# A gated-delta mixer: key norms from squares summed on TensorE ahead of the transposes, and raised priorities in the sample output

## The chip, the cores and the metric

The kernel runs on one core of a Trainium2 chip. A core has five engines with a queue of instructions each: TensorE (PE in the profile, its weight loads PEld), VectorE (DVE), ScalarE (ACT), GpSimd (POOL) and SyncE (SP), which here only issues DMAs. An engine runs its queue strictly in order and waits on semaphores for what other engines have to deliver. The metric is device time in microseconds (us) of one launch, as the median of several runs.

## The reference

The reference is one step of a small recurrent decoder trunk: two layers, each a feed-forward block, a mixer and a second feed-forward block, over 256 prompt tokens and 8 sequences of 8 sample tokens. The mixer's gated delta rule needs the keys normalised to unit length:

```python
def l2norm(x):
    return x * lax.rsqrt(jnp.sum(x * x, axis=-1, keepdims=True) + EPS)
...
    q = l2norm(qkv[:, :, 0]) * (DN_HEAD_DIM ** -0.5)
    k = l2norm(qkv[:, :, 1])
    v = qkv[:, :, 2]
    beta = jax.nn.sigmoid(scal[..., :DN_HEADS])
...
    kbeta = kb * bb[..., None]
    A = jnp.where(strict, jnp.einsum('nbhid,nbhjd->nbhij', kbeta, kb) * decay, 0.0)
...
        v_new = uc - jnp.einsum('bhcd,bhde->bhce', wc, S)
        o = jnp.einsum('bhcd,bhde->bhce', qc * jnp.exp(Gc)[..., None], S) + jnp.einsum('bhij,bhje->bhie', ac, v_new)
        gl = Gc[..., -1]
        S = S * jnp.exp(gl)[..., None, None] + jnp.einsum('bhcd,bhce->bhde', kc * jnp.exp(gl[..., None] - Gc)[..., None], v_new)
...
    o = rmsnorm(o, dn_norm_w) * jax.nn.silu(gates[..., RG_WIDTH:].reshape(B, L, DN_HEADS, DN_HEAD_DIM))
```

There are 4 heads of 128 columns; `g` are the decays, `G` their running sums, `o` the output that a second norm scales.

## The kernel before

All 320 tokens lie along the free dimension, the features on the 128 partitions. A product with a weight is done in three matmuls, since each operand is split into a rounded high part and a rest (`xh`, `xl`, `wh`, `wl`): L153, `Unit.mm`, eight blocks of 128 rows to a unit. A unit's weights come by one DMA (L117); ScalarE makes the high part (L125) and VectorE the rest (L130, the weight split).

TensorE's order is written out by hand. In the mixer the small dependent steps of the delta rule stand between pieces of the projections: `F(n)` issues the next n matmuls of the weight units as filler, `F.to(i)` those up to unit i, and the lists `FL`, `FZ`, `FY` hold the counts. When a unit is done, its `done` function reads its PSUM buffer out (a convolution for `k`, `q`, `v`: L667 and L668 on VectorE, then L677, L679, L700). There are three PSUM buffers for units (`mm`), four for the small steps (`sm`) and one for sums (`st`, the tile `ssp`).

The order on the other engines is made by a scheduler from priorities; `with tc.high_priority(offset=HPO)` (HPO is 400) puts what it holds ahead of other work. The order that it makes is fixed when the program is built, so an instruction that waits holds up all that stand behind it on its engine.

The steps that the change touches, in the order of the program, once in each layer:

- decays: TensorE's `gp` (L789 to L794) gives the running sums `G`; `gr` (L813, L816) gives them along rows; VectorE forms the differences `DN` (the program's `Dp`, L821) and `Ds` (L824), and ScalarE takes exponentials (L829 to L835);
- `tok`: TensorE transposes the keys (L850) in three groups, ScalarE squares each of ten blocks with its accumulator giving the sum of squares (L854), then copies the blocks scaled into `kd` (L858);
- norms: VectorE adds EPS (L868), GpSimd raises to the power -1/2 (L869), VectorE forms `dd` and `negc` (L870, L871), and later L872 and L873;
- `kk` and `kks`: products of keys (L885, L890), which VectorE scales into `nA` and `nAs` (L914, L921) for the triangular solve. Its steps are called `quads` (L907): TensorE multiplies, VectorE copies with a predicate (L1012) and transposes. The products for the queries (`kq_prep`) and the sums of `q` (L776) lie among them;
- output: `scale_o` squares `por` (its tile is `qa`), VectorE and GpSimd form the factor `fs` (L1050, L1051), ScalarE scales (L1056). For the sample tokens VectorE first adds `pso` and `kso` (L1158), which frees the PSUM buffer `pso`;
- state update: two halves of four products (L1194), each with the four `sm` buffers, and VectorE adds them to the state (L1197). Between the halves six matmuls of the next unit stand (`F(FL[19])`). After it the output is transposed (L1206).

A token (`self.token`, L722) is a tile of zeros that is handed on as a bias, to hold ScalarE's use of another function table until a certain step is done.

Of the kernel before, what the change touches and what calls it, by code (L numbers as in the profile page):

```python
# [11 lines left out]
AF = mybir.ActivationFunctionType  # L12
OP = mybir.AluOpType
# [13 lines left out]
EPS = 1e-6  # L27
# [3 lines left out]
HPO = 400  # L31
# [32 lines left out]
def bc(ap, n):  # L64
    return ap.to_broadcast([ap.shape[0], n])
# [11 lines left out]
def trunk(ctx, tc, x_prompt, x_sample, state_conv, state_rglru, state_delta,  # L77
# [6 lines left out]
    act, dve, pe, pool = nc.scalar.activation, nc.vector, nc.tensor, nc.gpsimd  # L84
    stt = dve.scalar_tensor_tensor
# [17 lines left out]
    def smtile():  # L103
        return smp.tile([128, 512], F32, name="sm")
# [504 lines left out]
    class Mixer:  # L609
# [127 lines left out]
        def run(self):  # L737
# [3 lines left out]
            vec, mhalf = C["vec"], C["mhalf"]  # L741
            ka, kas, qa, qas, va, vas = self.ka, self.kas, self.qa, self.qas, self.va, self.vas
# [12 lines left out]
            beta, g, ss, rk, negc, dd, kds, negEG, nk, t0_ = (sv[:, i] for i in range(10))  # L755
# [12 lines left out]
            ssp = sttile()  # L768

            def sumsq_units(c0, src, srcs, hs):  # L770
                for h in hs:
                    if h < NH:
                        s = sqtile()
                        act(s[:, 0:NP], src[:, h], AF.Square)
                        for t in range(2):
                            pe.matmul(ssp[:, c0 + 4 * t + h:c0 + 4 * t + h + 1], s[:, t * 128:(t + 1) * 128],  # L776
                                      ones[:, 0:1], start=True, stop=True)
                    else:
                        sx = tmp.tile([128, NH, 64], F32, name="sqs")
                        act(sx, srcs, AF.Square)  # L780
                        for p in range(2):
                            pe.matmul(ssp[:, c0 + 8 + p:c0 + 9 + p], sx[:, 2 * p:2 * p + 2].rearrange("p a b -> p (a b)"),
                                      ones[:, 0:1], start=True, stop=True)

            F(FL[1])
            self.late_state()
            F(FL[2])
            gp = smtile()
            pe.matmul(gp[:, 0:8], U, g[:, 0:8], start=True, stop=True)  # L789
            pe.matmul(gp[:, 8:10], U8, g[:, 8:10], start=True, stop=True)  # L790
# [6 lines left out]
            eG, eGL, eSel, eKD = GE[:, 0:10], GE[:, 10:20], GE[:, 20:52], GE[:, 52:62]  # L797
# [10 lines left out]
            for t in range(2):  # L808
                gr = smtile()
                grs.append(gr)  # L810
                for h in range(NH):
                    u = 4 * t + h
                    pe.matmul(gr[:, h * 128:(h + 1) * 128], bc(g[:, u:u + 1], 128), U, start=True, stop=True)  # L813
            gr = smtile()
            for p in range(2):
                pe.matmul(gr[:, 128 * p:128 * p + 128], bc(g[:, 8 + p:9 + p], 128), U8, start=True, stop=True)  # L816
            with tc.high_priority(offset=HPO):
                for t in range(2):
                    for h in range(NH):
                        u = 4 * t + h  # L820
                        stt(Dp[:, u], grs[t][:, h * 128:(h + 1) * 128], G[:, u:u + 1], mnP, op0=OP.subtract, op1=OP.min)  # L821
                for p in range(2):
                    for h, r in enumerate(HF):
                        stt(Ds[r, p], gr[r, 128 * p + 64 * h:128 * p + 64 * h + 64], G[r, 8 + p:9 + p], mn8[r],  # L824
                            op0=OP.subtract, op1=OP.min)
                if TK:
                    act(GE, GE, AF.Exp)
                else:
                    act(GE, GE, AF.Exp, bias=self.token(Ds[:, 1, 63:64]))  # L829
                dve.tensor_scalar(negEG, eG, -1.0, None, op0=OP.mult)  # L830
                act(Dp[:, 0:4], Dp[:, 0:4], AF.Exp)
                act(Dp[:, 4:8], Dp[:, 4:8], AF.Exp)
                act(Ds, Ds, AF.Exp)
                act(qg[:, :, 0:128], grs[1].rearrange("p (h i) -> p h i", h=NH), AF.Exp)
                act(qg[:, :, 128:192], gr[:, 0:256].rearrange("p (h i) -> p h i", h=NH), AF.Exp)  # L835
                self.tokq = self.token(qg[:, 3, 128:129])

            kd = mt([128, NU, 128], "kd")
            vn = mt([128, NU, 128], "vn")
            qss = mt([128, NU], "qss")  # L840

            def tok(u0, src, srcs, dst, scl, sums=None):
                n = 4 if u0 < 8 else 2
                ps = smtile()
                for i in range(n):
                    if u0 < 8:
                        a = src[:, i, 32 * u0:32 * u0 + 128]
                    else:
                        a = srcs[:, 2 * i:2 * i + 2]
                    pe.transpose(ps[:, i * 128:(i + 1) * 128], a, ident)  # L850
                if sums is not None:
                    with tc.high_priority(offset=HPO):
                        for i in range(n):
                            act(dst[:, u0 + i], ps[:, i * 128:(i + 1) * 128], AF.Square,  # L854
                                accum_out=sums[:, u0 + i:u0 + i + 1])
                for i in range(n):
                    u = u0 + i
                    act(dst[:, u], ps[:, i * 128:(i + 1) * 128], AF.Copy, scale=scl[:, u:u + 1])  # L858
# [3 lines left out]

            F(FL[4])
            for u0 in (0, 4, 8):
                tok(u0, ka, kas, kd, eKD, ss)
                F(FL[5])
            with tc.high_priority(offset=HPO):
                dve.tensor_scalar(ss, ss, EPS, None, op0=OP.add)  # L868
                pool.tensor_tensor(rk, ss, mhalf, op=OP.pow)  # L869
                dve.tensor_mul(dd, beta, rk)  # L870
                stt(negc, dd, -1.0, rk, op0=OP.mult, op1=OP.mult)  # L871
            dve.tensor_mul(dd, dd, rk)  # L872
            dve.tensor_mul(nk, ss, rk)  # L873

            nA = mt([128, 8, 128], "nA")
            at = mt([128, 8, 128], "at")
            nAs = mt([128, 2, 64], "nAs")
# [3 lines left out]
            for t in range(2):  # L881
                tk = slice(t * 128, t * 128 + 128)
                ps = smtile()
# [26 lines left out]
            with tc.high_priority(offset=HPO):  # L910
                for t in range(2):
                    for h in range(NH):
                        u = 4 * t + h
                        stt(nA[:, u], kk[t][:, h * 128:h * 128 + 128], negc[:, u:u + 1], Dp[:, u],  # L914
                            op0=OP.mult, op1=OP.mult)
# [75 lines left out]
            for li, s in enumerate(LEV[1:]):  # L991
# [16 lines left out]
                for a, b in grp:  # L1008
                    n = b - a
# [36 lines left out]
            def scale_o(u0, n):  # L1046
                for i in range(n):
                    act(sqtile()[:, 0:128], por[:, u0 + i], AF.Square, accum_out=oss[:, u0 + i:u0 + i + 1])
                us = slice(u0, u0 + n)
                stt(fs[:, us], oss[:, us], 1.0 / 128, qss[:, us], op0=OP.mult, op1=OP.add)  # L1050
                pool.tensor_tensor(fs[:, us], fs[:, us], mhalf[:, us], op=OP.pow)  # L1051
                for i in range(n):
                    if SO:
                        dve.tensor_scalar(por[:, u0 + i], por[:, u0 + i], fs[:, u0 + i:u0 + i + 1], None, op0=OP.mult)
                    else:
                        act(por[:, u0 + i], por[:, u0 + i], AF.Copy, scale=fs[:, u0 + i:u0 + i + 1])  # L1056
# [98 lines left out]
            for p in range(2):  # L1155
                u = 8 + p
                pe.matmul(pso[:, p * 128:p * 128 + 128], ats[:, p], vn[:, u], start=True, stop=True)
            dve.tensor_add(por[:, 8:10], pso[:, 0:256].rearrange("p (u c) -> p u c", c=128), kso[:, 1])  # L1158
            scale_o(8, 2)

            ves = []
# [251 lines left out]
```

## Time and profile before

| | |
|---|---|
| runs, us | 1306.49 median of 3 (1301.82 to 1308.19) |
| profiled execution, us | 1302.74, of which the span 1301.0 |
| busy: PE / DVE / ACT / POOL | 97% / 68% / 56% / 9% of the span |
| mean granted TensorE clock | 0.984 of full speed |
| HBM traffic | 143 GB/s over the span |

The span goes from the first instruction to the last. A row of a timeline gives the start, the duration, engine, line, operation, the tile written and those read, the shapes and a count; at its end stands, in brackets, how long the engine had been idle before and what released it. Neighbouring rows overlap, since an instruction's end is counted with its drain: what an instruction takes in a row of its kind is the distance from start to start. `sv` in the profile is a small tile for vectors: `ss`, `rk`, `dd`, `negc` and others.

### The profile page before, as it was taken

The numbers are of one execution on the slowest core, as the hardware profiler recorded it, in microseconds if no ns is written. First come the engines' busy times: TensorE is split into PE (matmuls) and PEld (weight loads), VectorE is DVE, ScalarE is ACT, GpSimd is POOL, SyncE is SP. The second block draws the span as 40 slices with busy tenths as digits, with TensorE's granted clock in tenths as the row PEclk, the third lists the DMA queues.
The fourth block names the chain that finished last, engine by engine and source line by source line (L and its number), as shares of the span: only waits on it lengthen the run. The fifth ranks groups of instructions, "written<-read, shape, count | busy, mean of one in ns | idle before, by whom it ended". The sixth has DMA issues, their size and how long they took to land.

```text
span 1301.0 us, 24528 instructions
## 1 busy us (share of the span) xinstructions
PE 1255.6 (97%) x9849; PEld 1220.4 (94%) x9849; DVE 885.6 (68%) x1542; ACT 730.6 (56%) x1216; POOL 117.9 (9%) x243
## 2 busy tenths in 40 slices
PE   7899999999999999999999999999999999999995
PEld 6899999889979999999999999999897899999995
DVE  5977744689777877764487775459995768767443
ACT  5655544575586755544465554446758666555444
POOL 1200000232120100000000000013321110000000
PEclk8999999999989999999999999999999899999998
DMA  7655555563336455555635555575332655555541
GB/s 180 163 160 162 157 154 162 141 163 82 83 96 188 125 163 162 163 150 165 182 105 163 162 162 153 159 200 132 82 87 70 173 143 162 163 162 158 147 134 41
DMA packets 355686, 187.26 MB, mean 144 GB/s; under 512 B 8890, under 2 KB 353292, under 8 KB 355572
## 3 DMA queue, kind: packets, MB, share of 16 engines
q1 hardware_dynamic: 352724, 178.51, 48.7%
q0 software_dynamic: 2672, 6.65, 1.9%
q8 instruction: 77, 1.26, 0.4%
q10 hardware_dynamic: 176, 0.53, 0.1%
q14 instruction: 37, 0.30, 0.1%
HBM read 179.16 MB, written 6.51 MB: 143 GB/s over the span
## 4 chain that ended last, share of the span: by engine, by line
PE 84%; DVE 7%; ACT 5%; DMA 2%; issue 1%; POOL 1%; SPq 0%; ACTq 0%; DVEq 0%
PE mm L153 41%; PE sm L153 35%; PE sm L907 2%; DVE xl L222 2%; ACT xh L221 1%; DMA raw<-in_ffn_w_up_dram 1%; PE st L226 1%; DVE wl L130 1%; ACT wh L125 1%; PE sm L1194 1%; PE sm L971 1%; DVE x L411 1%; DVE xr L1097 0%; ACT hp L1072 0%; DVE co L679 0%
## 5 line engine op out<-in xcount | busy, mean ns | idle before, releaser
L130 DVE TENSOR_TENSOR wl<-raw,wh 128x1024 fp32r<-128x1024 f32 (+1 forms) x322 | 385.3, 1197 | 208.2 <-ACT wh L125 204.2
L125 ACT ACTIVATE wh<-raw 128x1024 fp32r<-128x1024 f32 (+1 forms) x317 | 328.1, 1035 | 342.7 <-issue 130.3
L153 PE MATMUL mm<-xh,wl 128*128 128x320 f32 x976 | 294.4, 305 | 4.9 <-DVE wl L130 4.9
L153 PE MATMUL mm<-xh,wh 128*128 128x320 f32 x976 | 294.9, 305 | 1.1 <-ACT xh L221 1.1
L153 PE MATMUL mm<-xl,wh 128*128 128x320 f32 x976 | 286.7, 303 | 2.1 <-DVE xl L222 2.1
L153 PE MATMUL sm<-xh,wh 128*128 128x320 f32 x720 | 215.6, 299 | 0.0
L153 PE MATMUL sm<-xh,wl 128*128 128x320 f32 x720 | 215.5, 299 | 0.0
L153 PE MATMUL sm<-xl,wh 128*128 128x320 f32 x720 | 215.3, 299 | 0.0
L153 PEld LDWEIGHTS mm<-xh,wl 128*128 128x128 f32 x976 | 185.8, 191 | 7.9 <-DVE wl L130 5.9
L153 PEld LDWEIGHTS mm<-xh,wh 128*128 128x128 f32 x976 | 186.0, 191 | 6.0 <-issue 2.3
L153 PEld LDWEIGHTS mm<-xl,wh 128*128 128x128 f32 x976 | 183.3, 191 | 4.4 <-DVE xl L222 2.4
L153 PEld LDWEIGHTS sm<-xh,wl 128*128 128x128 f32 x720 | 136.1, 189 | 0.0
L153 PEld LDWEIGHTS sm<-xh,wh 128*128 128x128 f32 x720 | 136.1, 189 | 0.0
L153 PEld LDWEIGHTS sm<-xl,wh 128*128 128x128 f32 x720 | 136.1, 189 | 0.0
L153 PE MATMUL sm<-gh,wh 128*128 128x320 f32 x374 | 112.2, 300 | 0.0
L153 PE MATMUL sm<-gh,wl 128*128 128x320 f32 x374 | 111.9, 299 | 0.0
L153 PE MATMUL sm<-gl,wh 128*128 128x320 f32 x374 | 111.8, 299 | 0.0
L153 PE MATMUL mm<-gh,wh 128*128 128x320 f32 x330 | 99.0, 300 | 0.0
L153 PE MATMUL mm<-gh,wl 128*128 128x320 f32 x330 | 98.8, 300 | 0.0
L153 PE MATMUL mm<-gl,wh 128*128 128x320 f32 x330 | 98.7, 299 | 0.0
L497 ACT ACTIVATE gh<-t 128x320 fp32r<-128x320 f32 x88 | 70.0, 805 | 8.2 <-DVE t L495 7.3
L153 PEld LDWEIGHTS sm<-gh,wl 128*128 128x128 f32 x374 | 70.7, 189 | 0.0
(440 smaller groups left out, 2059.8 us busy)
## 6 DMA issues: line engine op xcount, KB each, us to landing
raw<-in_ffn_w_up_dram SPq DMA_DIRECT2D x176, 512.0 KB, 3.9
raw<-in_ffn_w_down_dram SPq DMA_DIRECT2D x64, 512.0 KB, 4.1
raw<-in_w_in_dram SPq DMA_DIRECT2D x48, 512.0 KB, 4.1
raw<-in_ffn_w_down_dram SPq DMA_DIRECT2D x32, 384.0 KB, 3.5
raw<-in_w_out_dram SPq DMA_DIRECT2D x16, 512.0 KB, 3.9
aux<-in_state_delta_dram SPq DMA_DIRECT2D x8, 512.0 KB, 6.5
out_dram<-aux POOLq DMA_DIRECT2D x8, 512.0 KB, 5.7
xtok<-in_x_prompt_dram SPq DMA_DIRECT2D x2, 512.0 KB
```

Source lines behind the costliest of these rows:

```text
L125: act(wh[:, :nk], raw[:, :nk], *((AF.Copy,) if tok is None or tok[0] else (AF.Identity, tok[1]())))
L130: (sub or dve).tensor_sub(wl[:, :nk], raw[:, :nk], wh[:, :nk].bitcast(F32))
L153: pe.matmul(self.blk.ps(), w, il(xx), start=self.first and self.pos == 1, stop=self.last and self.pos == 3 * self.nk)
L221: act(h, pr(x[:, k]), AF.Copy, scale=g)
L222: stt(il(xl[:, k]), pr(x[:, k]), g, h.bitcast(F32), op0=OP.mult, op1=OP.subtract)
L226: pe.matmul(ps[:, t:t + 1], s[:, a:b], ones[:, 0:1], start=start and t == 0, stop=stop, skip_group_check=True)
L411: dve.tensor_add(x[:, k], x[:, k], t)
L497: act(h, pr(t2), AF.Copy)
L907: pe.matmul(ps[HF[h], 64 * i:64 * i + 64], lhs(u, h), rhs(u, h), start=True, stop=True)
L971: pe.matmul(ps[32 * j:32 * j + 32, 128 * i:128 * i + 128], kz[:, h, i, c:c + 32], SS[p][:, j // 2, 4 * (j % 2) + b], start=b == 0, stop=b ...
L1194: pe.matmul(ps2[j], kd[r, u], ve[r], start=True, stop=True)
```

## The change

The sums of squares of the keys are no longer taken by ScalarE's accumulator from the transposed keys. `sumsq_units`, which the kernel already used for `q`, squares the keys as they come (ScalarE, L774 and L780) and sums over the partitions by matmuls with one column of ones. Heads 0 to 2 stand ahead of `gp`, head 3 and the sample tokens behind `gr`. The norms' small operations move up with them. The output factor's two operations and the sample output's add get the raised priority. No line of the diff concerns the state update itself.

```diff
--- before.py
+++ after.py
@@ -785,6 +785,7 @@
             F(FL[1])
             self.late_state()
             F(FL[2])
+            sumsq_units(0, ka, kas, (0, 1, 2))
             gp = smtile()
             pe.matmul(gp[:, 0:8], U, g[:, 0:8], start=True, stop=True)
             pe.matmul(gp[:, 8:10], U8, g[:, 8:10], start=True, stop=True)
@@ -814,6 +815,14 @@
             gr = smtile()
             for p in range(2):
                 pe.matmul(gr[:, 128 * p:128 * p + 128], bc(g[:, 8 + p:9 + p], 128), U8, start=True, stop=True)
+            sumsq_units(0, ka, kas, (3, 4))
+            with tc.high_priority(offset=HPO):
+                dve.tensor_scalar(ss, ssp[:, 0:10], EPS, None, op0=OP.add)
+                pool.tensor_tensor(rk, ss, mhalf, op=OP.pow)
+                dve.tensor_mul(dd, beta, rk)
+                stt(negc, dd, -1.0, rk, op0=OP.mult, op1=OP.mult)
+            dve.tensor_mul(dd, dd, rk)
+            dve.tensor_mul(nk, ss, rk)
             with tc.high_priority(offset=HPO):
                 for t in range(2):
                     for h in range(NH):
@@ -839,7 +848,7 @@
             vn = mt([128, NU, 128], "vn")
             qss = mt([128, NU], "qss")
 
-            def tok(u0, src, srcs, dst, scl, sums=None):
+            def tok(u0, src, srcs, dst, scl):
                 n = 4 if u0 < 8 else 2
                 ps = smtile()
                 for i in range(n):
@@ -848,11 +857,6 @@
                     else:
                         a = srcs[:, 2 * i:2 * i + 2]
                     pe.transpose(ps[:, i * 128:(i + 1) * 128], a, ident)
-                if sums is not None:
-                    with tc.high_priority(offset=HPO):
-                        for i in range(n):
-                            act(dst[:, u0 + i], ps[:, i * 128:(i + 1) * 128], AF.Square,
-                                accum_out=sums[:, u0 + i:u0 + i + 1])
                 for i in range(n):
                     u = u0 + i
                     act(dst[:, u], ps[:, i * 128:(i + 1) * 128], AF.Copy, scale=scl[:, u:u + 1])
@@ -862,16 +866,8 @@
 
             F(FL[4])
             for u0 in (0, 4, 8):
-                tok(u0, ka, kas, kd, eKD, ss)
+                tok(u0, ka, kas, kd, eKD)
                 F(FL[5])
-            with tc.high_priority(offset=HPO):
-                dve.tensor_scalar(ss, ss, EPS, None, op0=OP.add)
-                pool.tensor_tensor(rk, ss, mhalf, op=OP.pow)
-                dve.tensor_mul(dd, beta, rk)
-                stt(negc, dd, -1.0, rk, op0=OP.mult, op1=OP.mult)
-            dve.tensor_mul(dd, dd, rk)
-            dve.tensor_mul(nk, ss, rk)
-
             nA = mt([128, 8, 128], "nA")
             at = mt([128, 8, 128], "at")
             nAs = mt([128, 2, 64], "nAs")
@@ -1047,8 +1043,9 @@
                 for i in range(n):
                     act(sqtile()[:, 0:128], por[:, u0 + i], AF.Square, accum_out=oss[:, u0 + i:u0 + i + 1])
                 us = slice(u0, u0 + n)
-                stt(fs[:, us], oss[:, us], 1.0 / 128, qss[:, us], op0=OP.mult, op1=OP.add)
-                pool.tensor_tensor(fs[:, us], fs[:, us], mhalf[:, us], op=OP.pow)
+                with tc.high_priority(offset=HPO):
+                    stt(fs[:, us], oss[:, us], 1.0 / 128, qss[:, us], op0=OP.mult, op1=OP.add)
+                    pool.tensor_tensor(fs[:, us], fs[:, us], mhalf[:, us], op=OP.pow)
                 for i in range(n):
                     if SO:
                         dve.tensor_scalar(por[:, u0 + i], por[:, u0 + i], fs[:, u0 + i:u0 + i + 1], None, op0=OP.mult)
@@ -1155,7 +1152,8 @@
             for p in range(2):
                 u = 8 + p
                 pe.matmul(pso[:, p * 128:p * 128 + 128], ats[:, p], vn[:, u], start=True, stop=True)
-            dve.tensor_add(por[:, 8:10], pso[:, 0:256].rearrange("p (u c) -> p u c", c=128), kso[:, 1])
+            with tc.high_priority(offset=HPO):
+                dve.tensor_add(por[:, 8:10], pso[:, 0:256].rearrange("p (u c) -> p u c", c=128), kso[:, 1])
             scale_o(8, 2)
 
             ves = []
```

VectorE, layer 0, between the running sums and the next weight split; `sv<-st` (L820) adds EPS to the sums, `sv<-sv` at L822 and L823 are `dd` and `negc`. Before:

```order
L821 SCALAR_TENSOR_TENSOR DN_3175<-sm,G,mnP 128x128 [waits PE_49]
L821 SCALAR_TENSOR_TENSOR DN_3175<-sm,G,mnP 128x128 x3
L821 SCALAR_TENSOR_TENSOR DN_3175<-sm,G,mnP 128x128 [waits PE_49]
L821 SCALAR_TENSOR_TENSOR DN_3175<-sm,G,mnP 128x128 x3
L824 SCALAR_TENSOR_TENSOR Ds<-sm,G,mn_454 64x64 [waits PE_49]
L824 SCALAR_TENSOR_TENSOR Ds<-sm,G,mn_454 64x64 x3
L668 TENSOR_TENSOR cb<-mm,rsb_86 128x8x8
L722 TENSOR_SCALAR tok<-Ds 128x1 [waits DVE_49]
L130 TENSOR_TENSOR wl<-raw,wh 128x1024 [waits DMAHW7_49]
```

and after:

```order
L830 SCALAR_TENSOR_TENSOR DN_3187<-sm,G,mnP 128x128 [waits PE_49]
L830 SCALAR_TENSOR_TENSOR DN_3187<-sm,G,mnP 128x128 x3
L820 TENSOR_SCALAR sv<-st 128x10 [waits PE_49]
L830 SCALAR_TENSOR_TENSOR DN_3187<-sm,G,mnP 128x128
L822 TENSOR_TENSOR sv<-sv 128x10 [waits Pool_49]
L830 SCALAR_TENSOR_TENSOR DN_3187<-sm,G,mnP 128x128
L823 SCALAR_TENSOR_TENSOR sv<-sv 128x10 [waits DVE_49]
L830 SCALAR_TENSOR_TENSOR DN_3187<-sm,G,mnP 128x128 x2
L833 SCALAR_TENSOR_TENSOR Ds<-sm,G,mn_454 64x64 x4
L668 TENSOR_TENSOR cb<-mm,rsb_86 128x8x8
L722 TENSOR_SCALAR tok<-Ds 128x1 [waits DVE_49]
L130 TENSOR_TENSOR wl<-raw,wh 128x1024 [waits DMAHW7_49]
```

The add, `dd` and `negc` now stand inside the row of `DN`; `Ds`, L668, the token and the split L130 stand behind `dd`, which waits for GpSimd.

TensorE, layer 0, the keys' products `kk` (L885 before, L881 after) and the sample tokens' `kks` (L890 before, L886 after). Before:

```order
L885 MATMUL sm<-ka 128x128 [waits PE_49,Activation_49]
L885 MATMUL sm<-ka 128x128 x3
L885 MATMUL sm<-ka 128x128 [waits Activation_49]
L885 MATMUL sm<-ka 128x128 x3
L890 MATMUL sm<-ka 64x64 [waits DVE_49]
L890 MATMUL sm<-ka 64x64 x3
```

and after:

```order
L881 MATMUL sm<-ka 128x128 [waits Activation_49]
L881 MATMUL sm<-ka 128x128 x3
L881 MATMUL sm<-ka 128x128 [waits Activation_49]
L881 MATMUL sm<-ka 128x128 x3
L886 MATMUL sm<-ka 64x64 [waits Activation_49]
L886 MATMUL sm<-ka 64x64 x3
```

`kks` waited for VectorE (the buffer that `nA` reads) and now waits for ScalarE.

VectorE, layer 0, the sample section; `qa<-sm,kso` is the sample output's add, `hp` and `xr` belong to the other recurrence, `aux<-aux,sm` is the state update. Before:

```order
L1097 SCALAR_TENSOR_TENSOR xr<-vo,hp 128x320 [waits DVE_49,Pool_49]
L1090 TENSOR_TENSOR hp<-hp 128x320 [waits Activation_49] x2
L1094 TENSOR_TENSOR hp<-hp,ts__4325 128x8 [waits DVE_49]
L1093 TENSOR_TENSOR ts__4333<-vo,vec 128x8
L1090 TENSOR_TENSOR hp<-hp 128x320 [waits Activation_49]
L1097 SCALAR_TENSOR_TENSOR xr<-vo,hp 128x320 [waits DVE_49,Pool_49]
L1094 TENSOR_TENSOR hp<-hp,ts__4333 128x8 [waits DVE_49]
L1093 TENSOR_TENSOR ts__4341<-vo,vec 128x8
L1158 TENSOR_TENSOR qa<-sm,kso 128x256 [waits PE_49]
L1097 SCALAR_TENSOR_TENSOR xr<-vo,hp 128x320 [waits DVE_49,Pool_49]
L1094 TENSOR_TENSOR hp<-hp,ts__4341 128x8 [waits DVE_49]
L130 TENSOR_TENSOR wl<-raw,wh 128x1024 [waits DMAHW1_49,Activation_49]
```

and after:

```order
L1091 TENSOR_TENSOR hp<-hp,ts__4327 128x8 [waits DVE_49]
L1094 SCALAR_TENSOR_TENSOR xr<-vo,hp 128x320 [waits DVE_49,Pool_49]
L1087 TENSOR_TENSOR hp<-hp 128x320 [waits Activation_49] x2
L1156 TENSOR_TENSOR qa<-sm,kso 128x256 [waits PE_49]
L1091 TENSOR_TENSOR hp<-hp,ts__4335 128x8 [waits DVE_49]
L1090 TENSOR_TENSOR ts__4343<-vo,vec 128x8
L1087 TENSOR_TENSOR hp<-hp 128x320 [waits Activation_49]
L1094 SCALAR_TENSOR_TENSOR xr<-vo,hp 128x320 [waits DVE_49,Pool_49]
L1091 TENSOR_TENSOR hp<-hp,ts__4343 128x8 [waits DVE_49]
L1090 TENSOR_TENSOR ts__4351<-vo,vec 128x8
L130 TENSOR_TENSOR wl<-raw,wh 128x1024 [waits DMAHW1_49,Activation_49]
L1047 SCALAR_TENSOR_TENSOR fs<-oss,qss 128x4 [waits Activation_49]
```

The add has moved up, ahead of four small operations, one of 320 columns and a scan.

## Rows read from the trace of the kernel before

**Rows 1.** TensorE's waits, whole trace: engine, tile, line, releaser: us, times, longest
```profile
PE sm L890 <- DVE nA L914: 4.7, 2, 2.4
PE sm L1194 <- DVE qa L1158: 4.3, 2, 2.2
```

**Rows 2.** TensorE's timeline, layer 0: start, us, engine, line, operation, count, idle before
```profile
281.53 0.38 PE L153 MATMUL mm<-xh,wh 128*128 128x320 f32 x1
...
284.50 0.30 PE L153 MATMUL mm<-xh,wh 128*128 128x320 f32 x1
285.23 0.40 PE L153 MATMUL mm<-xh,wl 128*128 128x320 f32 x1 [0.43 <-DVE wl L130]
...
288.71 2.17 PE L885 MATMUL sm<-ka 128*128 128x128 f32 x16
293.25 0.57 PE L890 MATMUL sm<-ka 128*64 128x64 f32 x8 [2.37 <-DVE nA L914]
...
298.85 1.15 PE L907 MATMUL sm<-Tt,nA 64*64 64x64 f32 x32
```

**Rows 3.** VectorE's timeline, the same stretch
```profile
280.48 2.16 DVE L821 SCALAR_TENSOR_TENSOR DN<-sm,G,mnP 128x128 f32<-128x128 f32 x8
...
283.95 1.22 DVE L130 TENSOR_TENSOR wl<-raw,wh 128x1024 fp32r<-128x1024 f32 x1
...
288.67 0.17 DVE L868 TENSOR_SCALAR sv<-sv 128x10 f32<-128x10 f32 x1
...
291.21 0.19 DVE L870 TENSOR_TENSOR sv<-sv 128x10 f32<-128x10 f32 x1 [1.89 <-POOL sv L869]
...
302.94 0.57 DVE L679 SCALAR_TENSOR_TENSOR co<-cb,vec,co 128x344 f32<-128x344 f32 x1 [0.57 <-ACT co L677]
303.86 0.92 DVE L1012 COPY_PREDICATED Tt<-mT,sm 128x512 f32<-128x512 int32 x2 [0.35 <-PE sm L907]
```

**Rows 4.** GpSimd's timeline, the norms' power
```profile
288.93 2.24 POOL L869 TENSOR_TENSOR sv<-sv,mhalf 128x10 f32<-128x10 f32 x1 [0.67 <-DVE sv L868]
```

**Rows 5.** Windows: us, busy PE, PEld, DVE, ACT, POOL, clock, DMA share, GB/s
```profile
293.00:297.00 4.00, 3.75 (x21) 3.63 (x22) 3.91 (x13) 3.51 (x9) 0.00 (x0) 0.57 0.00 0
303.00:345.00 42.00, 42.00 (x650) 38.67 (x647) 38.98 (x101) 20.37 (x39) 11.46 (x25) 1.00 0.34 90
```

**Rows 6.** TensorE's timeline, four passes of L776 and what follows
```profile
312.72 0.50 PE L776 MATMUL st<-ones,sq 128*128 128x1 f32 x4
313.15 1.08 PE L971 MATMUL sm<-aux,hp 128*32 128x128 f32 x32
```

**Rows 7.** TensorE's timeline, layer 1, the same place as rows 2
```profile
922.63 0.45 PE L890 MATMUL sm<-ka 128*64 128x64 f32 x8 [2.37 <-DVE nA L914]
...
926.60 1.15 PE L907 MATMUL sm<-Tt,nA 64*64 64x64 f32 x32
...
929.08 0.40 PE L153 MATMUL mm<-xh,wl 128*128 128x320 f32 x1 [0.45 <-DVE wl L130]
```

**Rows 8.** ScalarE's timeline, scaled copies of the transposed keys
```profile
293.63 1.64 ACT L858 ACTIVATE kd<-sm,GE 128x128 f32<-128x128 f32 x6
```

**Rows 9.** VectorE's timeline, layer 0, sample section
```profile
377.04 0.16 DVE L1094 TENSOR_TENSOR hp<-hp,ts__4325 128x8 f32<-128x8 f32 x1
...
378.48 0.41 DVE L1158 TENSOR_TENSOR qa<-sm,kso 128x256 f32<-128x256 f32 x1
```

**Rows 10.** TensorE's timeline, sample section of layer 0, then layer 1
```profile
375.67 1.13 PE L1194 MATMUL sm<-nA,kd 32*128 32x512 f32 x6
...
391.67 0.38 PE L1206 MATMUL sm<-ident,qa 128*128 128x128 f32 x2
...
1004.17 1.13 PE L1194 MATMUL sm<-nA,kd 32*128 32x512 f32 x6
...
1011.39 3.77 PE L1194 MATMUL sm<-at,kd 32*128 32x512 f32 x8 [1.80 <-DVE aux L1197]
...
1021.63 0.38 PE L1206 MATMUL sm<-ident,qa 128*128 128x128 f32 x2
```

## Prediction

> **What bounds the kernel now.** I read the shares of busy time first: TensorE is busy for 97% of the span, so the time is TensorE's instructions plus its waits, and every edit is worth what it adds to or takes from that chain. Next come TensorE's waits over the whole trace. Few are left, and two of those shown belong to the lines that the diff touches: L890 waits 4.7 us in two pieces for VectorE's `nA`, and L1194 waits 4.3 us in two pieces for VectorE's add of L1158 [rows 1]. Layer 0's mixer, in TensorE's timeline, shows the first place: behind the first transposes of `ka` a new weight unit at 284.50, whose second matmul waits 0.43 for its weight split, then products `kk` at 288.71, and then 2.37 us of idle before `kks` at 293.25 [rows 2]. VectorE's timeline tells why: the sums of squares reach VectorE at 288.67 (L868), after ScalarE's Squares; L870 takes up the power at 291.21, and `nA` follows, which frees the PSUM buffer that `kks` needs [rows 3]. The power itself takes GpSimd 2.24 us [rows 4]. So from L868's start to L870's start a power costs VectorE's chain 291.21 - 288.67 = 2.54 us. The windows show two more things: during 293 to 297 the granted clock is 0.57, after a wait that found it at full speed, and from 303 to 345 VectorE is busy for 38.98 of 42 us [rows 5]. There VectorE has no slack: whatever makes it late before 303 stays late until 345.
>
> **The change, part by part.** All times are layer 0's; layer 1 repeats the order.
>
> (a) The sums on TensorE. Added are ten matmuls of one column. Such a matmul is there already: four cost 313.15 - 312.72 = 0.43 us, 0.1075 per pass or 0.215 per fp32 matmul with two passes [rows 6], where x4 counts passes. Six of them stand ahead of the `gp` products and four behind `gr`: 12 x 0.1075 = 1.29 and 8 x 0.1075 = 0.86, together 2.15 us on TensorE per layer. Bounds for the whole: 20 passes at the 0.057 us that the `kks` passes take (layer 1's eight in 0.45, [rows 7]) give 1.1, at twice the row 4.3; I take the row, since it is the same line L776.
>
> The Trainium skill (TensorE: Matmul & The Clock Gate, Wait -- 56ns) gives a short matmul a floor near 25 ns from start to start; by it the twenty passes would be some 0.5 us, an estimate. The row of 0.1075 disagrees, and it decides here.
>
> (b) The Squares taken from ScalarE. Ten pairs of Square and accumulator read go, the last of them just ahead of the `kd` copies; five wider Squares come. ScalarE is not what TensorE waits for here, until `kks`: that wait moves from `nA` to a `kd` copy of L858 (the order shows the releaser change). Bounds: 0 to the 2.37 now idle.
>
> (c) The norms' small operations, moved up on VectorE. Here I find the cost. In VectorE's new order the add of EPS stands after four of the eight `DN` operations, one `DN` follows, and then `dd`, which waits for the power. Behind `dd` in the queue stand three `DN`, four `Ds`, L668 (which frees a PSUM buffer for TensorE's next unit), the token and the weight split L130. Before, none of these had a power ahead of them: the eight `DN` ran from 280.48 at 0.26 each (2.16 / 8), to 282.56; `Ds`, L668 and the token took the 1.39 from there to the split at 283.95 [rows 3]. Now: the `gr` products, which end at 281.53 where the fillers go on [rows 2], end 1.29 later at 282.82, the last four sums' passes at 283.68, and the add starts some 0.2 later, 283.86. `dd` is then at 283.86 + 2.54 = 286.40. `dd`, `negc` and three `DN` come to 0.1 + 0.1 + 0.78, and with the same 1.39 behind them the split starts at about 288.78, 4.83 later than 283.95, L668 just ahead. TensorE reaches the unit's first matmul at 284.50 + 2.15 = 286.65 and waits to 288.85 for L668's buffer (2.2), then from 288.99 to 290.06 for the split (1.07). That is 3.27 us of new idle in place of 0.43: +2.84 per layer.
>
> The power has then run, so the 2.37 us ahead of `kks` goes. TensorE gets there at 288.71 + 4.83 + 2.17 = 295.71. ScalarE's `kd` copies, six of them at 293.63 before [rows 8], need the exponentials that wait for `Ds`'s token at 288.72; then four copies, a table load of 1.28, two activations for `qa` and three more copies end at about 295.75. So about 0 is left of that wait; up to 1 us if ScalarE is late.
>
> Sum of (a) to (c) in layer 1: 2.15 + 2.84 - 2.37 = +2.62. Layer 0 had also lost time to the clock: from `kks` to the `quads` (L907) it took 298.85 - 293.25 = 5.60, in layer 1 926.60 - 922.63 = 3.97 [rows 2, 7]. Of these 1.63 us layer 1 gives 0.45 back, idle at the next weight split [rows 7], so at most 1.18 can be won: +1.44.
>
> That is not all, since VectorE itself is late for the same work: 4.83 at the split, less the 1.89 that it idled at L870 and idles no more [rows 3], is 2.9. Ahead of the predicated copy into `Tt` (L1012) it has 0.57 + 0.35 = 0.92 of slack, L679 and the idle [rows 3], which leaves 2.0, and the new order puts two products of `kq_prep` ahead of that copy, up to 1.1 us by L679's 0.57. With VectorE full until 345 this 2.0 to 3.1 stays, as far as TensorE waits for VectorE's steps there: I take 2.2 in layer 0, where TensorE comes 1.44 late by itself, and 3.1 in layer 1, where it comes 2.62 late. These stand instead of 1.44 and 2.62: **+5.3** in all.
>
> Clock: the new idle of 2.2 and 1.07 can bring a stretch at the lower level of 1.2 GHz (0.57 of granted clock in 293:297 is mostly that) as the old 2.37 did in one of two layers, at 1.18 net. 0 to 1.18 per layer; the new idle comes in two shorter pieces, so I take **+0.7** for both layers together.
>
> (d) Sample output. L1158 moves four to six instructions up in VectorE's queue; it started at 378.48, and in the new order it stands where L1094 started at 377.04 [rows 9], 1.44 sooner. The wait of some 2.15 ahead of the state products of L1194 [rows 1] shortens to 0.7. But the second half of those products needs the buffers that the four adds of L1197 free, and these stand behind the same scans, splits and token on VectorE as before: layer 1 waits there 1.80 on an add [rows 10]. VectorE's sum up to that add is the same. So 0, with bounds -1.44 and 0 per layer; and the lower clock level, at which these eight run (3.77 us against 1.13 for six, [rows 10]), may reach further into the end of layer 0's section, as it does in layer 1: between the first product of L1194 and the last of L1206 layer 1 needs 1021.63 - 1004.17 = 17.46, layer 0 391.67 - 375.67 = 16.0 [rows 10], so 0 to +1.45: take **+0.4**.
>
> The power of `fs` now stands earlier, ScalarE's scaling some 1.7 sooner, and no wait of TensorE hangs on it: 0. GpSimd's queue: the norm power passes small copies of `nct` and `cb`, which wait for L668 anyway, and the `fs` power the copies of `rgl`; no DMA issue is passed by either, none is moved on SP. 0.
>
> Sum: 5.3 + 0.7 + 0.4 = +6.4. The profiled execution took 1302.74 us (span 1301.0 and 1.74 around it): 1309.1. The median of the runs, 1306.49, is 3.75 above it; with the same +6.4 it becomes **1313**.
>
> **The rivals.** *Not slower.* If GpSimd's power ends before VectorE reaches `dd`, or VectorE has enough else to do, the split isn't late, and only passes stand against the old wait: 2 x (2.15 - 2.37) - 1.18 = -1.6, or 1305; with L1158's release paying in full, 2 x 1.44 more, 1302. It decides from the point where `dd` starts 2.8 us earlier than I have it, when TensorE's wait at the split is the old 0.43. For it: VectorE idles 1.89 at L870 now, so the same pair need not cost more than that. Against: four `DN` of cover are all used up before the add.
>
> *Clock stays low.* Both new waits drop the clock, and the state update runs its half-clock stretch longer: 2 x 1.18 + 1.45 in place of my 1.1, +9.1 in all: 1316. For it, 0.57 in one layer after 2.37 us of idle; against, layer 1 kept its clock after the same idle [rows 7].
>
> *Nothing of the third part.* No line of the diff splits the state update: its six fillers between the halves stand in both programs. If raised priorities only reorder work of equal length, the time is 1306.
>
> **How the numbers follow.** Forecast 0.67, not slower 0.17, low clock 0.12, nothing 0.04. What this kernel's measurement can tell from no change is 0.5%, 6.5 us: 1300.0 to 1313.0. The forecast's own range, 1306 to 1319 (ScalarE's copies late by 1 us per layer and passes at twice the row at the upper end, no clock drop and VectorE recovering half by 345 at the lower), straddles the upper bound: 0.32 same, 0.35 slower. "Not slower" is same with 0.11 and faster with 0.06. Low clock is slower with 0.11 and same with 0.01, nothing is same: faster 0.06, same 0.48, slower 0.46. The range of 1303.5 to 1320 leaves out the better part of "not slower" and what a low clock would add to that upper end.
>
> **What would show it.** Right: `dd` idle some 2.3 us on GpSimd within the `DN` row, the split near 288.8, TensorE idle for about 3.3 us at the unit after the first transposes, no wait at `kks`, `quads` 2 to 3 us later. Wrong: `dd` without idle, the split within 1.5 us of its old place relative to TensorE, or VectorE making up its delay by 345; then the first rival holds. L1194's wait near 0.7 with the second half unmoved confirms (d).

## The result, and the profile after

The changed kernel takes 1314.28 us (median, 1313.53 to 1314.33); the kernel before took 1305.7 beside it. The ratio is 1.0068 [1.0052, 1.0083]: slower by 0.7%. The forecast was 1313, with VectorE held up by the power as its largest step.

TensorE's waits in the changed kernel, whole trace (engine, tile, line, releaser: us, times, longest):

```profile
PE sm L1192 <- DVE aux L1195: 6.5, 2, 3.2
...
PE sm L925 <- ACT qa L700: 3.6, 2, 1.8
PE mm L153 <- DVE tok L722: 3.5, 2, 1.7
...
PE sm L1192 <- DVE qa L1156: 1.4, 2, 0.7
```

The wait of L890 [rows 1] is gone. New are 3.5 us for the token (it stands for L668, one row ahead of it on VectorE) and 3.6 us for `qa`; the wait for the sample output's add fell from 4.3 to 1.4, and 6.5 us stand at the second half of the state products, where [rows 10] show 1.80 in layer 1 alone.

TensorE's timeline of the kernel before at the places that are compared below: the first product of `gp` in either layer, the second step's `quads`, the first transposes of `ka` in layer 1:

```profile
276.82 0.28 PE L789 MATMUL sm<-sv,U 128*128 128x8 f32 x2
...
283.65 0.60 PE L850 MATMUL sm<-ident,ka 128*128 128x128 f32 x4
...
302.67 1.15 PE L907 MATMUL sm<-PY,Nt 64*64 64x64 f32 x32
```

```profile
906.21 0.28 PE L789 MATMUL sm<-sv,U 128*128 128x8 f32 x2
...
913.04 0.60 PE L850 MATMUL sm<-ident,ka 128*128 128x128 f32 x4
```

And of the changed kernel, layer 0. The twelve passes now stand where `gp` stood, at 279.05, 2.23 us later than 276.82: in this execution the clock had fallen near 48 us, in the first feed-forward block, behind a wait that both kernels have (3.61 us here, 3.60 before; over 48 to 52 us the granted clock is 0.50 here and 1.00 before). That much is to be taken off each start in layer 0:

```profile
279.05 1.40 PE L776 MATMUL st<-ones,sq 128*128 128x1 f32 x12
280.31 0.37 PE L790 MATMUL sm<-sv,U 128*128 128x8 f32 x2
...
288.12 0.60 PE L859 MATMUL sm<-ident,ka 128*128 128x128 f32 x4
...
288.83 0.30 PE L153 MATMUL mm<-xl,wh 128*128 128x320 f32 x1
290.87 0.40 PE L153 MATMUL mm<-xh,wh 128*128 128x320 f32 x1 [1.75 <-DVE tok L722]
292.06 0.40 PE L153 MATMUL mm<-xh,wl 128*128 128x320 f32 x1 [0.79 <-DVE wl L130]
...
297.61 0.45 PE L886 MATMUL sm<-ka 128*64 128x64 f32 x8
...
301.58 1.15 PE L903 MATMUL sm<-Tt,nA 64*64 64x64 f32 x32
...
307.61 0.49 PE L925 MATMUL sm<-qa,ka 128*128 128x128 f32 x2 [1.80 <-ACT qa L700]
308.03 1.15 PE L903 MATMUL sm<-PY,Nt 64*64 64x64 f32 x32
```

VectorE, GpSimd and ScalarE in the same stretch, the first two to be read against [rows 3, 4]:

```profile
286.17 0.17 DVE L820 TENSOR_SCALAR sv<-st 128x10 f32<-128x10 f32 x1 [1.00 <-PE st L782]
...
288.45 0.17 DVE L822 TENSOR_TENSOR sv<-sv 128x10 f32<-128x10 f32 x1 [1.85 <-POOL sv L821]
...
290.80 1.21 DVE L130 TENSOR_TENSOR wl<-raw,wh 128x1024 fp32r<-128x1024 f32 x1
```

```profile
286.43 1.99 POOL L821 TENSOR_TENSOR sv<-sv,mhalf 128x10 f32<-128x10 f32 x1 [2.04 <-DVE sv L820]
```

```profile
307.05 0.51 ACT L700 ACTIVATE qa<-co,tok 128x256 f32<-128x256 f32 x1 [1.18 <-DVE co L679]
```

The add waits 1.00 for the last sums, `dd` 1.85 for the power, and the split, behind both, starts at 290.80. TensorE stands 1.75 us for L668's buffer and 0.79 for the split. At 297.61 `kks` starts without a wait. At 307.61 TensorE waits 1.80 us for `qa`, which ScalarE's L700 brings late, itself waiting for VectorE's L679.

Layer 1 is the same, but for the clock. TensorE's timeline there, and two windows (us, busy PE, PEld, DVE, ACT, POOL, clock, DMA share, GB/s):

```profile
911.99 1.40 PE L776 MATMUL st<-ones,sq 128*128 128x1 f32 x12
...
916.97 2.53 PE L814 MATMUL sm<-U,sv 128*128 128x128 f32 x16
...
922.72 0.60 PE L859 MATMUL sm<-ident,ka 128*128 128x128 f32 x4
```

```profile
912.00:915.00 3.00, 3.00 (x28) 3.00 (x27) 0.91 (x4) 0.81 (x3) 0.65 (x3) 0.96 0.52 133
915.00:919.00 4.00, 4.00 (x22) 4.00 (x21) 2.31 (x8) 3.38 (x7) 0.72 (x3) 0.60 0.15 42
```

Behind the twelve passes and the products of `gp`, with no idle between (TensorE is busy for 4.00 of 4.00 us), the granted clock falls: 0.60 over 915 to 919, most of it at the 1.2 GHz level, until it comes back within `gr`.

The sample section of layer 0, and the last row of layer 1's, TensorE:

```profile
381.05 1.13 PE L1192 MATMUL sm<-nA,kd 32*128 32x512 f32 x6
382.88 1.12 PE L1192 MATMUL sm<-nA,kd 32*128 32x512 f32 x2 [0.70 <-DVE qa L1156]
...
388.25 3.77 PE L1192 MATMUL sm<-at,kd 32*128 32x512 f32 x8 [3.23 <-DVE aux L1195]
...
397.80 0.38 PE L1204 MATMUL sm<-ident,qa 128*128 128x128 f32 x2
```

```profile
1032.55 0.38 PE L1204 MATMUL sm<-ident,qa 128*128 128x128 f32 x2
```

From the first sum or `gp` product to the last L1206, the section took 114.85 us in layer 0 and 115.42 in layer 1 before (start 276.82 and 906.21, ends in [rows 10]); now 397.80 - 279.05 = 118.75 and 1032.55 - 911.99 = 120.56. That is 3.90 + 5.14 = 9.04 us. The profiled spans differ by 10.8: these 9.04 and the 2.23 of the first block, less some 0.5 elsewhere.

### The profile page after: what moved, and what is told of

Same layout as the page of the kernel before. It is cut to its first block, busy times and chain, and to the rows that moved or that the text cites. A ratio compares the mean times of both kernels' runs of the same rounds, so it can differ in the third digit from the quotient of the medians.

```text
span 1311.8 us, 24577 instructions
## 1 busy us (share of the span) xinstructions
PE 1262.3 (96%) x9889; PEld 1227.2 (94%) x9889; DVE 886.6 (68%) x1542; ACT 729.1 (56%) x1186; POOL 119.4 (9%) x243
## 3 DMA queue, kind: packets, MB, share of 16 engines
q8 instruction: 77, 1.26, 0.4%
## 4 chain that ended last, share of the span: by engine, by line
PE 84%; DVE 8%; ACT 5%; DMA 1%; issue 1%; POOL 1%; SPq 0%; ACTq 0%; DVEq 0%
PE mm L153 41%; PE sm L153 35%; PE sm L903 2%; DVE wl L130 1%; DVE xl L222 1%; PE st L226 1%; DMA raw<-in_ffn_w_up_dram 1%; ACT xh L221 1%; ACT wh L125 1%; DVE co L679 1%; PE sm L967 1%; DVE xr L1094 1%; PE sm L1192 1%; PE st L776 0%; ACT hp L1069 0%
## 5 line engine op out<-in xcount | busy, mean ns | idle before, releaser
L130 DVE TENSOR_TENSOR wl<-raw,wh 128x1024 fp32r<-128x1024 f32 (+1 forms) x322 | 385.4, 1198 | 209.7 <-ACT wh L125 205.6
```

Of the source, the lines that this page charges most:

```text
L130: (sub or dve).tensor_sub(wl[:, :nk], raw[:, :nk], wh[:, :nk].bitcast(F32))
```

## The experiments

All are timed in five rounds; the kernel before took 1305.27 beside e1 to e4 and 1304.87 beside e5 to e8. Intervals of the ratio to it in brackets. The theory: VectorE's queue, held by the power, costs most; the passes cost their rows; the sample part nothing. The rivals: the passes and their clock alone, or a gain in the sample part that something hides.

**e1, the norms' part alone.** The two priorities of the output go back:

```diff
-                with tc.high_priority(offset=HPO):
-                    stt(fs[:, us], oss[:, us], 1.0 / 128, qss[:, us], op0=OP.mult, op1=OP.add)
-                    pool.tensor_tensor(fs[:, us], fs[:, us], mhalf[:, us], op=OP.pow)
+                stt(fs[:, us], oss[:, us], 1.0 / 128, qss[:, us], op0=OP.mult, op1=OP.add)
+                pool.tensor_tensor(fs[:, us], fs[:, us], mhalf[:, us], op=OP.pow)
...
-            with tc.high_priority(offset=HPO):
-                dve.tensor_add(por[:, 8:10], pso[:, 0:256].rearrange("p (u c) -> p u c", c=128), kso[:, 1])
+            dve.tensor_add(por[:, 8:10], pso[:, 0:256].rearrange("p (u c) -> p u c", c=128), kso[:, 1])
```

> The changed kernel with the output factor and the sample output's add at their old priority: the norms' part alone. My theory: the sample part is worth nothing, since the second half of the state products waits for VectorE's adds whichever way, so the time is that of the whole change, 1314.3 us within 1, with the waits at the state products back at 2.1 and about 1.8. Rival: the earlier release pays its 1.44 us in each layer and the norms cost more; then this one is 1317.

Measured: 1314.25, ratio 1.0076 [1.0062, 1.0089]; waits 2.1 per layer at the fourth product of the first half (its passes are the seventh and eighth, hence "seventh" in e2's expectation), 2.8 together at the second half. As far as the intervals tell, the whole loss is in the norms' part.

Its profiled execution shows something of the clock that the changed kernel's doesn't. TensorE in layer 0, and two windows (columns as above):

```profile
276.88 1.40 PE L776 MATMUL st<-ones,sq 128*128 128x1 f32 x12
...
288.70 0.40 PE L153 MATMUL mm<-xh,wh 128*128 128x320 f32 x1 [1.74 <-DVE tok L722]
...
307.07 0.49 PE L925 MATMUL sm<-qa,ka 128*128 128x128 f32 x2 [1.77 <-ACT qa L700]
...
382.10 1.13 PE L1190 MATMUL sm<-nA,kd 32*128 32x512 f32 x6
```

```profile
291.00:295.00 4.00, 4.00 (x20) 3.96 (x19) 3.53 (x8) 3.97 (x9) 1.08 (x4) 0.57 0.78 202
308.00:312.00 4.00, 4.00 (x41) 3.88 (x38) 4.00 (x11) 1.33 (x3) 1.72 (x3) 0.57 0.35 105
```

The waits are those of the changed kernel, but here the clock falls behind both; there the granted clock is 1.00 over the same two windows. The first state product comes 382.10 - 276.88 = 105.22 us behind the first pass, in the changed kernel 381.05 - 279.05 = 102.00: with the two falls it is 3.22 us more. In layer 1 of e1 neither wait has such a fall.

**e2, the output's part alone**, the same lines put into the kernel before.

> The kernel before with only the output factor and the sample output's add at raised priority. My theory: 1305.7 us within 1; the wait of TensorE at the seventh state product goes from 2.1 to 0.7 in each layer and comes back at the second half (3.2). Rival: 1302.8, each layer 1.44 shorter.

Measured: 1305.6, ratio 1.0000 [0.9988, 1.0013]. Its waits show where the 1.44 us go:

```profile
PE sm L1196 <- DVE aux L1199: 6.5, 2, 3.2
...
PE sm L1196 <- DVE qa L1160: 1.4, 2, 0.7
```

0.7 per layer at the fourth product, and 3.2 at the second half, which waits for VectorE's adds to the state: given back in full at the very next product.

**e3, `dd` behind `Ds`.** Add and power stay:

```diff
-                dve.tensor_mul(dd, beta, rk)
-                stt(negc, dd, -1.0, rk, op0=OP.mult, op1=OP.mult)
-            dve.tensor_mul(dd, dd, rk)
-            dve.tensor_mul(nk, ss, rk)
...
                 tok(u0, ka, kas, kd, eKD)
                 F(FL[5])
+            with tc.high_priority(offset=HPO):
+                dve.tensor_mul(dd, beta, rk)
+                stt(negc, dd, -1.0, rk, op0=OP.mult, op1=OP.mult)
+            dve.tensor_mul(dd, dd, rk)
+            dve.tensor_mul(nk, ss, rk)
```

> The changed kernel with the add of EPS and the power where they are, but dd and negc written behind the transposes, so that on VectorE dd stands behind all of DN and Ds instead of between them. My theory (VectorE's row held up by the power is the larger part of the loss): the weight split starts some 2 us earlier, TensorE's waits of 1.75 and 0.79 at the unit behind the first transposes shrink to about 0.5 together, the wait for qa of 1.8 goes too; 2 us per layer less, 1310 us. Rival (the passes on TensorE and their clock are what costs, VectorE's delay is covered): 1314 still.

Measured: 1306.63, ratio 1.0016 [1.0003, 1.0029]: 1314.28 - 1306.63 = 7.65 us of the 9 are gone, more than the 4 that I expected. VectorE in layer 0:

```profile
285.71 0.17 DVE L820 TENSOR_SCALAR sv<-st 128x10 f32<-128x10 f32 x1 [1.00 <-PE st L782]
...
286.83 1.17 DVE L829 SCALAR_TENSOR_TENSOR Ds<-sm,G,mn 64x64 f32<-64x64 f32 x4
288.03 0.17 DVE L868 TENSOR_TENSOR sv<-sv 128x10 f32<-128x10 f32 x1
...
288.51 1.22 DVE L130 TENSOR_TENSOR wl<-raw,wh 128x1024 fp32r<-128x1024 f32 x1
```

`dd` (L868) no longer idles, and the split starts 288.51 - 285.71 = 2.80 behind the add, where it was 4.63. The place of four small instructions on VectorE is the larger part of the result. In the profiled executions of both kernels the clock falls behind the passes in layer 1 alone, so the rival, that the passes and their clock are what costs, falls. TensorE:

```profile
289.78 0.40 PE L153 MATMUL mm<-xh,wl 128*128 128x320 f32 x1 [0.87 <-DVE wl L130]
...
295.71 0.45 PE L887 MATMUL sm<-ka 128*64 128x64 f32 x8 [0.50 <-ACT kd L858]
...
303.05 1.11 PE L926 MATMUL sm<-qa,ka 128*128 128x128 f32 x8
```

The wait for L668's buffer is gone, 0.87 is left at the split, 0.50 at `kks` for ScalarE's `kd`, and `qk` (L926) waits for nothing. The expectation listed the wait for `qa` and didn't count it: the first state product comes 3.50 us sooner behind the first pass than in the changed kernel (377.09 - 278.59 = 98.50 against 102.00), 1.44 of it by `kks` (295.71 - 278.59 = 17.12 against 18.56), the rest where `qk` waited.

**e4, the sums added and not used**: the kernel before with the two `sumsq_units` lines and nothing else; the norms come by the old way.

> The kernel before, with the twenty passes of the sums added on TensorE (and their five Squares on ScalarE) and their result not used; norms come by the old way. My theory: passes cost what a row of them shows, 2.15 us per layer, and push the old chain behind them, so 1305.7 + 4.3 = 1310 us, up to 1.7 more for each layer in which the clock falls behind the passes. Rival: they are taken up by the 2.37 us that TensorE waits ahead of kks, and the time is 1306.

Measured: 1310.02, ratio 1.0031 [1.0015, 1.0047]: 4.75 us by the medians, 4.0 by the ratio (2.0 to 6.1 by its interval). TensorE, layer 0:

```profile
278.51 1.40 PE L776 MATMUL st<-ones,sq 128*128 128x1 f32 x12
...
296.48 0.60 PE L892 MATMUL sm<-ka 128*64 128x64 f32 x8 [2.37 <-DVE nA L916]
```

The wait of 2.37 stands as before, so it doesn't take the passes up; from the first pass to `kks` it is 17.97 against 16.43, so that 1.54 of 2.15 us reach this point; most of the rest is the old 0.43 at the split, which is gone. The sections of the two profiled executions are only 1.52 and 1.03 us longer than before, the medians say more: that the passes reach the end is shown, how much of 4.3 us does isn't.

**e5, the add late too.** As e3, and the add of EPS behind `Ds`:

```diff
                 self.tokq = self.token(qg[:, 3, 128:129])
+            with tc.high_priority(offset=120):
+                dve.tensor_scalar(ss, ssp[:, 0:10], EPS, None, op0=OP.add)
+            with tc.high_priority(offset=HPO):
+                pool.tensor_tensor(rk, ss, mhalf, op=OP.pow)
...
+            with tc.high_priority(offset=60):
+                dve.tensor_mul(dd, beta, rk)
+                stt(negc, dd, -1.0, rk, op0=OP.mult, op1=OP.mult)
```

> As e3, and the add of EPS behind Ds as well (priority 120), dd and negc behind the second weight split (priority 60): VectorE waits neither for the last sums nor for the power. My theory (what VectorE waits for ahead of the split is what counts): VectorE's idle of 1.0 at the add goes, the wait of 0.87 at the split goes to about 0.4, 0.5 us per layer: 1305.6. Rival: after e3 the rest is the passes alone; 1306.6 still.

Measured: 1303.91, ratio 0.9996 [0.9987, 1.0005], 2.7 us under e3 (2.6 by the ratios, the runs beside them being others) where 1 was expected. The waits at the split and for L668 are both gone, some 0.6 at `kks` for ScalarE is left; so the whole of VectorE's part is undone, and passes and the old wait stand about even.

**e6, the sums behind gp.** As e5, heads 0 to 2 behind the nine fillers:

```diff
-            sumsq_units(0, ka, kas, (0, 1, 2))
             gp = smtile()
...
             F(FL[3])
+            sumsq_units(0, ka, kas, (0, 1, 2))
```

> As e5_add_late_too, with the sums of heads 0 to 2 behind the nine fillers that follow gp, so that the passes of one column don't stand in one row with the small products of gp. My theory (the clock's fall in layer 1 behind that row comes from the row's small products): TensorE keeps its full clock between gp and gr in layer 1, 1.3 us less, and VectorE gets G 1.3 earlier: about 1304. Rival: the clock falls all the same, as it does at other places by chance; 1305.6.

Measured: 1303.64, ratio 0.9993 [0.9979, 1.0007]: no difference that these runs tell. The clock did what the theory asked. The stretch with `gp` and `gr` of layer 0, e5 and then e6:

```profile
280.00:285.00 5.00, 5.00 (x32) 5.00 (x30) 3.31 (x12) 4.01 (x8) 0.71 (x3) 0.67 0.07 21
```

```profile
280.00:285.00 5.00, 5.00 (x45) 5.00 (x45) 3.60 (x13) 4.55 (x12) 0.71 (x4) 1.00 0.12 34
```

In e5 the clock fell there in both layers, in e6 in neither. In layer 0 the first state product comes 375.98 - 276.92 = 99.06 us behind the first of the sums and `gp` products in e5 and 374.56 - 277.17 = 97.39 in e6, 1.67 us less; in layer 1 it is 1.48 less. What it is worth over many executions stays open: the medians differ by 0.3 us.

**e7, squares in bfloat16.** As e5; the key squares are rounded to bfloat16 and summed with a column of bfloat16 ones, one pass each:

```diff
+                        s = sqtile()[:, 0:NP // 2].bitcast(mybir.dt.bfloat16)
+                        act(s, ka[:, h], AF.Square)
+                        for t in range(2):
+                            pe.matmul(ssp[:, 4 * t + h:4 * t + h + 1], s[:, t * 128:(t + 1) * 128],
+                                      ones_b, start=True, stop=True)
...
```

> As e5_add_late_too, with the key squares rounded to bfloat16, so that each of the ten sums is one pass on TensorE instead of two. My theory (the passes' number is what the sums cost): 1.07 us less per layer, of which e4 showed some 0.7 to reach the end: 1304. Rival: the row's cost is not in the passes (weights of 128 columns are loaded for each matmul all the same): 1305.6.

Measured: 1300.33, ratio 0.9975 [0.9963, 0.9987], 3.6 us under e5. TensorE, layer 0:

```profile
278.51 0.50 PE L777 MATMUL st<-ones_b,sq 128*128 128x1 bf16 x6
278.92 0.36 PE L806 MATMUL sm<-sv,U 128*128 128x8 f32 x2
...
283.78 0.19 PE L777 MATMUL st<-ones_b,sq 128*128 128x1 bf16 x2
283.84 0.19 PE L783 MATMUL st<-ones_b,sq 128*128 128x1 bf16 x2
```

Six passes take 0.41 where twelve took 1.26: not only half as many, each is 0.068 in place of 0.105. With the four others TensorE has some 1.6 us less to do per layer; the expected 1.07 counted the passes alone. It is not shown that the 1.8 per layer of the medians comes from this. In the rows a wait of 0.44 at the split is back and the one at `kks` is 0.78, and beside e6, where the clock is full too, the first state product gains only 0.8 per layer (375.09 - 278.51 = 96.58 against 97.39 in layer 0). The clock is a rival that this run doesn't separate, since it fell behind the passes in both layers of e5 and in neither of e7. The price of the gain is precision: the squares are rounded before they are summed.

**e8, the three together.**

> The three together: add and dd late, sums of heads 0 to 2 behind gp's fillers, squares in bfloat16. My theory: the gains of e6 and e7 add up, 1302.5, and it is faster than the kernel before (1305.3) by 0.2%. Rival: TensorE then waits again for VectorE's nA ahead of kks, or for ScalarE's kd copies, and it is 1304 to 1305.

Measured: 1298.76, ratio 0.9962 [0.9949, 0.9974]: faster than both kernels, 6.1 us under the one before, and 3.7 under what I expected. Two of its waits:

```profile
PE mm L153 <- DVE wl L130: 5.1, 5, 3.6
...
PE sm L904 <- ACT kd L875: 1.3, 2, 0.7
```

Of the first, 3.6 is the wait in the first feed-forward block that all kernels have, and 0.44 per layer stands at the split behind the first transposes, as before the change; `kks` waits 0.65 per layer for ScalarE. So the rival's condition holds, its price of 1304 to 1305 doesn't.

## Why the prediction was right

**The passes (a).** Forecast 2.15 per layer; the transposes of `ka` start 288.12 - 283.65 - 2.23 = 2.24 later in layer 0, and twelve passes took 1.26 against 1.29. e4 shows 1.54 of it reaching `kks`.

**VectorE's queue (c).** With 2.23 added, the forecast starts were 286.09 for the add, 288.63 for `dd` and 291.01 for the split; measured 286.17, 288.45 and 290.80. The power took 1.99 where [rows 4] had 2.24. The forecast counts TensorE's idle from start to start, while the brackets of 1.75 and 0.79 count from the end of a row: without waits it would have gone on 0.14 behind the row ahead of each, at 288.97 and 291.01, so it lost 1.90 + 1.05 = 2.95 against 3.27. The buffer came 0.2 sooner and TensorE 0.1 later than worked out. The old 0.43 is a bracket too, 0.59 from start to start, so the forecast's +2.84 is 0.16 too high by its own figures (its split is 4.83 later and 2.37 goes, which is 2.46 and not 2.62). `kks` waits for nothing, as forecast, and starts 297.61 - 293.25 - 2.23 = 2.13 later. e3 is the test: with `dd` behind `Ds` that loss is gone but for 0.87 at the split.

**VectorE late until 345.** The kind was right and the size too small. At the first `quads` layer 0 is only 301.58 - 298.85 - 2.23 = 0.50 later, since the 1.63 that it had lost to the clock don't recur; at the second step's `quads` it is 308.03 - 302.67 - 2.23 = 3.13 later, where I took 2.2. The place was wrong: it isn't the predicated copy behind `kq_prep` that makes TensorE wait, but `qk`, one step earlier, 1.80 us for `qa`. Once it had waited, nothing more came: at the first state product layer 0 is 381.05 - 375.67 - 2.23 = 3.15 later. Layer 1 is 1015.65 - 1004.17 - 5.78 = 5.70 later there, 1.7 of it by the clock, so some 4.0 where I took 3.1.

**The clock.** I gave 0.7 us to the new idle. In the profiled execution of the changed kernel the clock stayed at full speed behind both new waits in both layers; in e1, with the same norms' part, it fell behind both in layer 0, with 3.22 us more. So the mechanism exists, in one layer of the four profiled, and the term differs from execution to execution. What the prediction had at nothing is another fall, where TensorE had no idle: behind the twelve passes and `gp`, in layer 1, it cost some 1.7 (the transposes of `ka` are 922.72 - 913.04 = 9.68 later, of which 911.99 - 906.21 = 5.78 came in with the layer and 2.15 are the passes). Nor does one execution tell what the old wait cost: behind the 2.37 us ahead of `kks` the clock fell in five of the six layers profiled with it (one of the kernel before, both of e2 and of e4), where the forecast counted one of two.

**The sample part (d).** 0.70 left at the fourth product and 3.23 at the second half: the wait moved, as forecast, and e2 has it at 1.0000. The end of layer 0's section, at the lower clock, came 0.75 later still, in the forecast's 0 to 1.45; that of layer 1 came 0.56 sooner, so 0.2 in both where I took 0.4.

**The sum.** 6.4 forecast; measured 8.6 beside the first runs of the kernel before, 9.0 against the later ones and 9.04 in the profiled sections: layer 0 3.90 against 2.2, layer 1 5.14 against 3.1, and 1.1 for the clock in both. That 1313 came out within 1.3 us is in part luck: the three runs first shown of the kernel before had a median 1.2 to 1.6 us above that of its later runs. The mis-sized terms are VectorE's delay, by some 0.9 in each layer, where `qk` waits for `qa`, and the clock behind the passes, which had no term.

**The rivals.** "Not slower" named its condition, a split that isn't late, and its price, 1305: e5 brings the condition about, by moving `dd` behind the split, and takes 1303.91. In the changed kernel it doesn't hold. "Clock stays low" is seen behind the new waits in e1's layer 0 alone. "Nothing of the third part" is out by the interval.

## What to carry to other kernels

An instruction that waits for a slow engine costs what stands behind it in the same queue: before raising a priority, read what is queued behind the wait, and put the waiting instruction where its operand is ready. Moving a step off one engine pays only if the engine that gets it isn't the bound: on a TensorE at 97% the twenty passes, 2.15 us, about ate the 2.37 us that they freed (e5), and only when they were made cheaper was anything won. A wait shortened ahead of a fixed sum of another engine's work comes back at the next place that needs that work.

## What the runs showed of the hardware

The granted clock fell behind a row of small products without any idle in the engine (0.60 over 915 to 919 us in the changed kernel, 0.67 over 280 to 285 in e5, TensorE busy throughout): with all twelve fp32 passes right ahead of `gp` it fell at that place in the profiled executions of the changed kernel and of e1 and e3 in one layer of two and of e5 in both, and of e4 in none; with the sums behind the fillers (e6), or in bfloat16 (e7, e8), and without them, in none. That is five of ten layers against none of ten: it points to the small products, and chance isn't excluded. Behind real idle it was no surer: the same waits of 1.74 and 1.77 us left the clock at full speed in three layers of four (both of the changed kernel, one of e1) and not in the fourth, and a wait of 2.37 us left it there in one of six.
